# Dividing the softmax's weights before their transposition, instead of the attention's outputs

## The chip, the cores and the metric

One core of one Trainium2 chip. The metric is the device time of one execution in microseconds (us), as the median of three runs. Of the core's engines, TensorE (PE in the profile) multiplies matrices and transposes, VectorE (DVE) and ScalarE (ACT) work element by element and both read PE's results from PSUM, GpSimd (POOL) works element by element on SBUF, and SyncE (SP) starts the transfers of the weights. Each engine runs its own queue of instructions in order and waits at semaphores for the others.

## What is computed

Two transformer blocks in float32 over 512 positions of width 1024: a first block with a convolution branch, an attention with 16 heads of 64 and a feed-forward part, and a second block of two layers, one with a masked softmax attention over selected keys, one with a stick-breaking attention. The change touches the softmax of the first two attentions. Cut to that, the reference is

```
# first attention: a bias by distance, three dilated windows merged into one softmax
scores = q @ k.T - slopes * dist          # masked
m = max(scores);  p = exp(scores - m);  den = sum(p)
o = (p @ v) / den
y_b = o @ w_attn_out                      # later multiplied by a sigmoid gate

# second attention: keys selected per query
p = softmax(where(selected, q @ k.T * 0.125, -inf))
o = p @ v
y = (o * silu(g)) @ w_out_a
```

## The kernel before

Matrix products in float32 are made of three products of halves: each operand is split into a high and a low part (`h`, `l`; names ending in h and l or hi and lo), and PE runs h x h, l x h and h x l. ACT writes the high part, DVE or GpSimd subtracts it to get the low one. For weights that is `whi` on ACT and `wlo` on GpSimd (lines 119 and 123).

An attention runs over 8 pairs of heads (`pair_loop`). The queue of PE is written out by hand and goes along in slots, one for each head. In a slot PE computes, for four tiles of 128 queries, the scores of the present head (`scores`, lines 579 and 582: two products into one of two PSUM banks `s`, of 128, 256, 384 and 512 keys), the transpositions of the head before (`turn`, line 593: ten transpositions of 128x128 in three groups, into three banks `pt`), and the products of that earlier head's weights with the values (`weigh`, line 512, into the single bank `o`). Between any two of these steps stand some products of the projections for the pair after next (`pe.pull`; lines 301 to 303 and 325 to 327), which fill the time in which DVE and ACT work on the scores.

The element-wise work of a head and tile of queries: DVE takes scores and bias and writes the sum to `P` and its maximum to `nm` (line 626, one operation and a one-column read of its accumulator); ACT does the exponential in place and sums it to `den` (line 192). After the transposition ACT copies the high half to `PTh` (line 595), DVE subtracts it from `pt` to get `PTl` (line 596). When both heads of a pair are weighted, `joined` adds the two halves of `o` (ACT's copy at 518, DVE's addition at 519) into `f`.

The weights `P` are not divided by their sums. For each pair `widen` takes the reciprocals of the 2 x 4 columns of `den` (line 632) and spreads each over 64 columns of a tile `wide` (634), `denominators` transposes that tile with four PE transpositions into a bank `pt` (639), and ACT copies it to `rb`, times 0.5 (641). Then `finish` multiplies the outputs by it: in the first attention at line 943, into `o32`; in the second, line 1477 first multiplies the gate `gs` into `rb`, and 1478 the result into `f`. The 0.5 belongs to gates that are kept as twice their value.

The order on PE is fixed by the program's text. On DVE, ACT and GpSimd a scheduler decides the order when the kernel is built.

Of the kernel before, what the change touches and what calls it, by code (L numbers as in the profile page):

```python
# [10 lines left out]
F32 = mybir.dt.float32  # L11
F32R = mybir.dt.float32r
I32 = mybir.dt.int32
AF = mybir.ActivationFunctionType
OP = mybir.AluOpType
# [5 lines left out]
ND = D // 128  # L21
NT = S // 128
# [11 lines left out]
OFF = (0, 128, 384, 768)  # L34
# [11 lines left out]
FIRST = (2, 2, 3, 5)  # L46
DRAIN = (4, 1, 1, 2, 1, 1, 3)
# [101 lines left out]
def model_kernel(ctx: ExitStack, tc: tile.TileContext, x, norm1_g, w_in, gate_b, conv_w, conv_b, conv_norm_g,  # L149
                 w_conv_out, q_norm_g, k_norm_g, w_attn_out, w_out, norm2_g, w_up, ffn_conv_w, ffn_conv_b,  # L150
                 w_down, w_in_a, w_out_a, w_in_b, w_out_b, ln_g, ln_b, rope_c, rope_s, out, dbg=None):
    nc = tc.nc
# [18 lines left out]
    def ps_t():  # L171
        return ps("pt", 3)
# [42 lines left out]
    ident = const.tile([128, 128], F32, name="ident")  # L215
# [207 lines left out]
    with tc.tile_pool(name="rows", bufs=1) as rows, tc.manual_schedule(engines={  # L423
# [21 lines left out]
        for r in range(2):  # L445
            a = slice(64 * r, 64 * r + 64)
# [9 lines left out]
        p = ps_o()  # L456
# [43 lines left out]
    def tmp(pool):  # L500
        return pool.tile([128, S], F32, name="tmp", bufs={"dsa": 5, "loop1": 5, "loop3": 2, "glu": 3}[pool.name])
# [61 lines left out]
    class HeadPair:  # L563
# [2 lines left out]

        def __init__(self, tmps, pool, qk, v):
            self.tmps, self.pool, self.qk, self.v = tmps, pool, qk, v
            self.P, self.parts, self.o = {}, {}, {}

        def scores(self, r, qt):
            qs, (ks, kl) = self.qk
# [25 lines left out]
        def weigh(self, r, group):  # L598
            first, last = group == GROUPS[0], group == GROUPS[-1]
            if first:  # L600
                self.o[r] = ps_o()
            parts = {kt: self.parts[r, kt] for kt in group}
            values(self.o[r], self.v(), r, parts, group, first, last)
            if last:
                if r == 0:
                    self.f = tmp(self.tmps)
                joined(self.o[r], self.f, r)
                if r:
                    self.ended()

        def widen(self):
            pass

        def denominators(self):
            pass

    class SoftmaxPair(HeadPair):
        def __init__(self, tmps, pool, qk, v, bias, finish, scale=1.0):
# [5 lines left out]
        def weights(self, r, qt, n, sc, pp):  # L624
# [1 line left out]
            nc.vector.tensor_tensor_reduce(out=pp, in0=sc, in1=self.bias(r, qt), scale=-self.scale, scalar=3.0e38,  # L626
                                           op0=OP.add, op1=OP.min, accum_out=m)
            act(pp, pp, AF.Exp, bias=m, scale=-1.0, accum_out=d)

        def widen(self):  # L630
            rinv = self.pool.tile([128, 2, NT], F32, name="rinv", bufs=2)
            nc.vector.reciprocal(rinv, self.den)
            self.wide = tmp(self.tmps).rearrange("p (t r d) -> p t r d", t=NT, r=2)
            nc.vector.tensor_copy(self.wide, rinv.rearrange("p r t -> p t r")[:, :, :, None].to_broadcast([128, NT, 2, 64]))

        def denominators(self):
            pb = ps_t()
            for qt in range(NT):
                nc.tensor.transpose(pb[:, 128 * qt:128 * qt + 128], self.wide[:, qt].rearrange("p a b -> p (a b)"), ident)
            self.rb = tmp(self.tmps)  # L640
            nc.scalar.activation(self.rb, pb, AF.Copy, scale=0.5)

        def ended(self):
            self.finish(self.f, self.rb)

    class StickPair(HeadPair):

# [18 lines left out]
    def pair_loop(pair, stream_of, pulls, last=lambda: None):  # L666


        def slot(head, turns, weighs, widen, pulls):
            def step(fn):  # L670
                if fn is not None:
                    fn()
                    pe.pull(pulls.pop(0))

            pulls = list(pulls)
            score = [lambda qt=qt: head[0].scores(head[1], qt) for qt in range(NT)] if head else [None] * NT
            step(score[0])
            step(turns[0])
            step(score[1])
            step(turns[1])  # L680
            step(score[2])
            step(turns[2])
            step(weighs[0])
            step(score[3])
            step(weighs[1])
            step(weighs[2])
            if widen:
                widen()

        turns = weighs = [None] * 3  # L690
        for c in range(ND):
            stream_of(c)
            pr = pair(c)
            for r in range(2):
                slot((pr, r), turns, weighs, pr.widen if r else None, pulls[2 * c + r - 2 * ND] if c >= ND - 2 else pulls[0] if c or r else FIRST)
                turns = [(lambda g=g, r=r, pr=pr: pr.turn(r, g)) for g in GROUPS]
                weighs = [(lambda g=g, r=r, pr=pr: pr.weigh(r, g)) for g in GROUPS]
                if r:
                    weighs[1] = lambda pr=pr: (pr.weigh(1, GROUPS[1]), pr.denominators())
        last()  # L700
        pe.pull(DRAIN[0])
        slot(None, turns, weighs, None, DRAIN[1:])

    def value_tiles(pool, w, col, acts, puts):

# [80 lines left out]
    with tc.tile_pool(name="mix1", bufs=1) as mix1:  # L786
# [119 lines left out]
        with tc.tile_pool(name="loop1", bufs=1) as lp:  # L906
# [31 lines left out]
                pe.add(w_in, 0, 8, 3072 + 128 * c, hT, normed(1, kg))  # L938
                values_of(c, lp, w_in, 4096, hT, heads)

            def finish1(c):
                def finish(f, rb):
                    nc.vector.tensor_mul(o32[:, c, :], f, rb)
                return finish

            def pair1(c):
                B = []
                for r in range(2):
                    b = lp.tile([128, S], F32, name="B", bufs=2)
                    slope = 2.0 ** (-8.0 * (2 * c + r + 1) / NH)  # L950
                    nc.vector.scalar_tensor_tensor(b, dist, -float(np.float32(slope)), lnc, op0=OP.mult, op1=OP.add)
                    B.append(b)
                if c == ND - 1:
                    biased.add("last")
                    for fn in ready:
                        fn()
                    ready.clear()
                qk = heads.pop(c)
                return SoftmaxPair(lp, lp, (qk[0], qk[1]), lambda: qk["v"], lambda r, qt: B[r][:, 384 - 128 * qt:], finish1(c))

            ready = []

# [185 lines left out]

        return [(product or whole)(w, col + 128 * c, acts, done(c)) for c in cs]

    def gated(pool, into, f, c, already, scale=1.0):

        def parts():
            if not already:
                nc.vector.tensor_mul(f, f, gs[c])
            h, l = act_pair(pool, "og", ND)
            nc.scalar.activation(h, f, AF.Copy, scale=scale)
            nc.vector.scalar_tensor_tensor(l, f, scale, f32(h), op0=OP.mult, op1=OP.subtract)
            into.append((h, l))

        if already or c in gs:
            parts()
        else:
            waiting[c] = parts
# [199 lines left out]
    with tc.tile_pool(name="dsa", bufs=1) as dp:  # L1364
# [101 lines left out]
        with tc.tile_pool(name="loop2", bufs=1) as lp:  # L1466
            for g in gprods[3:]:
                pe.skewed(g)
            heads2(0)
            pe.finish()  # L1470
            heads2(1)
            pe.pull(LEAD[1] - 24)

            def finish2(c):
                def finish(f, rb):
                    if c in gs:
                        nc.vector.tensor_mul(rb, gs[c], rb)
                    nc.vector.tensor_mul(f, f, rb)
                    gated(dp, og, f, c, c in gs)
                return finish  # L1480

            def pair2(c):
                qk = heads.pop(c)
                return SoftmaxPair(dp, lp, (qk[0], qk[1]), lambda: qk["v"],
                                   lambda r, qt: maskb[:, OFF[qt]:OFF[qt] + 128 * (qt + 1)], finish2(c), 0.125)

            def stream2(c):
                if c + 2 < ND:
                    heads2(c + 2)
                elif c + 2 == ND:  # L1490
                    outs.append(Between(w_out_a, og, xS, kept))
                    outs[0].early()
                else:
                    outs[0].next()

            pair_loop(pair2, stream2, PULLS[1], lambda: outs[0].late())
            pe.finish()
            act_tables(LN_EXP)
# [9 lines left out]
    with tc.tile_pool(name="stick", bufs=1) as dp:  # L1508
        heads = {}
        og = []  # L1510
# [18 lines left out]
        with tc.tile_pool(name="loop3", bufs=1) as lp:  # L1529
            act_tables("sigmoid_and_others")  # L1530

            def pair3(c):
                qk = heads.pop(c)
                return StickPair(lp, lp, (qk[0], qk[1]), lambda: qk["v"], lambda f: gated(dp, og, f, c, False, 0.5))

            def last_e():
                es.append(dp.tile([128, S], F32, name="e", bufs=ND - 1) if es else keep.tile([128, S], F32, name="rc2"))
                return es[-1]

            es = []  # L1540

            def stream3(c):
                if c + 2 < ND:
                    heads3(lp, c + 2)
                    for g in gprods[slice(*GATES3[c + 2])]:
                        pe.skewed(g)
                elif c + 2 == ND:
                    outs.append(Last(w_out_b, og, xS, last_e))
                    outs[1].early()
                else:  # L1550
                    outs[1].next()

            heads3(lp, 0)
            heads3(lp, 1)
            pe.pull(LEAD[2])
            pair_loop(pair3, stream3, PULLS[2], lambda: outs[1].late())
            pe.finish()
            act_tables(LN_EXP)
# [27 lines left out]
```

## Time and profile before

| what | value |
|---|---|
| median of three runs | 1601.13 us (1597.56 to 1601.93) |
| profiled execution: its time | 1601.03 us |
| its span, first to last instruction | 1598.9 us |
| first attention's pairs | about 202 to 405 us |
| second attention's pairs | about 1046 to 1232 us |

The profile is of one execution, and its span lies 2.1 us inside that execution's time. Busy times are unions per engine; PE's instructions overlap one another, so their start times tell more than their lengths. A row by stretches gives the stretch's bounds and length in us, then the busy time and the number of instructions of PE, of PE's weight loads (PEld), of DVE, ACT and POOL, the granted share of PE's full clock, the share of the DMA engines and GB/s. A row of a group gives line, engine, operation, tiles and shapes with their count, then the busy time in us and the mean of one in ns, then the idle time ahead of them and what ended it. A row of the chain gives start and length in us.

### The profile page before, as it was taken

To read this page: it belongs to the slowest core of one execution; us is meant where nothing else is said; L and a number is where in the kernel's file an instruction comes from. 1 tells how busy PE (TensorE), PEld (TensorE's weight loads), DVE (VectorE), ACT (ScalarE), POOL (GpSimd) and SP (SyncE) were. 2 spreads that over 40 slices of the span, in tenths; PEclk is the share of its full clock that TensorE was granted. 3 is DMA by queue.
4 is the path that set the end of the run, shared out by engine and by line. 5 is a ranking of instruction groups with operands and counts; after the bars stand their busy time and mean duration, and the time that the engine had idled before them with its cause. 6 is when DMAs were issued, how large, how long until landed. Compare 5 with 4: busy or idle time off the path is not lost.

```text
span 1598.9 us, 21378 instructions
## 1 busy us (share of the span) xinstructions
PE 1527.2 (96%) x7870; PEld 1296.7 (81%) x7870; DVE 1121.4 (70%) x1837; ACT 845.4 (53%) x1524; POOL 806.5 (50%) x680
## 2 busy tenths in 40 slices
PE   7999799998999999999999999999999789999996
PEld 6877688887878888888888887888887678888885
DVE  8998777776166467727735669988887765777764
ACT  4455787777552444424333444366766345666652
POOL 3789944332744653454444474445442875334324
PEclk9999899999999999999999999999999899999998
DMA  4323212221233423343333242322220313212212
GB/s 149 88 87 98 86 54 73 60 67 40 67 105 105 126 86 92 93 118 91 90 110 89 84 125 66 80 80 66 67 67 14 92 40 106 67 54 80 67 52 80
DMA packets 234604, 130.37 MB, mean 82 GB/s; under 512 B 5206, under 2 KB 232774, under 8 KB 234500
## 3 DMA queue, kind: packets, MB, share of 16 engines
q1 hardware_dynamic: 234356, 128.75, 27.7%
q8 instruction: 62, 1.02, 0.3%
q14 instruction: 42, 0.34, 0.1%
q10 hardware_dynamic: 144, 0.26, 0.0%
HBM read 126.90 MB, written 2.10 MB: 81 GB/s over the span
## 4 chain that ended last, share of the span: by engine, by line
PE 57%; DVE 23%; ACT 7%; POOL 5%; issue 5%; DMA 2%; DVEq 0%; SPq 0%; ACTq 0%; POOLq 0%
PE pj L301 10%; PE pj L302 9%; PE pj L303 9%; PE s L302 5%; PE s L303 5%; PE s L301 5%; DVE pt L831 5%; PE o L512 2%; POOL wlo L123 2%; PE pt L593 2%; PE pj L325 2%; PE pj L327 2%; PE pj L326 2%; POOL S L837 2%; DVE score L1442 1%
## 5 line engine op out<-in xcount | busy, mean ns | idle before, releaser
L123 POOL TENSOR_TENSOR wlo<-wraw,whi 128x256 fp32r<-128x256 f32 (+2 forms) x548 | 653.8, 1218 | 684.4 <-ACT whi L119 639.0
L301 PE MATMUL pj<-Ah,whi 128*128 128x512 f32 (+3 forms) x896 | 362.2, 404 | 15.2 <-DVE v L718 9.8
L119 ACT CAST whi<-wraw 128x1024 fp32r<-128x1024 f32 (+3 forms) x255 | 243.8, 965 | 224.3 <-PE pj L302 82.1
L303 PE MATMUL pj<-Ah,wlo 128*128 128x512 f32 (+3 forms) x896 | 350.4, 391 | 2.5 <-POOL wlo L123 2.5
L302 PE MATMUL pj<-Al,whi 128*128 128x512 f32 (+3 forms) x896 | 350.7, 391 | 0.0
L301 PEld LDWEIGHTS pj<-Ah,whi 128*128 128x128 f32 (+1 forms) x896 | 171.2, 191 | 41.9 <-issue 9.1
L303 PEld LDWEIGHTS pj<-Ah,wlo 128*128 128x128 f32 (+1 forms) x896 | 170.3, 190 | 39.1 <-POOL wlo L123 3.4
L302 PEld LDWEIGHTS pj<-Al,whi 128*128 128x128 f32 (+1 forms) x896 | 171.1, 191 | 24.4
L301 PE MATMUL s<-Ah,whi 128*128 128x512 f32 (+1 forms) x352 | 135.8, 386 | 4.0 <-ACT Ah L1298 4.0
L302 PE MATMUL s<-Al,whi 128*128 128x512 f32 (+1 forms) x352 | 135.7, 386 | 3.6 <-DVE Al L1299 3.6
L303 PE MATMUL s<-Ah,wlo 128*128 128x512 f32 (+1 forms) x352 | 135.6, 385 | 1.0 <-POOL wlo L123 1.0
L831 DVE SCALAR_TENSOR_TENSOR pt<-S,cw,pt 128x496 f32<-128x496 f32 (+19 forms) x180 | 124.8, 738 | 6.4 <-ACT pt L824 3.8
L325 PE MATMUL pj<-whi,Ah 128*128 128x256 f32 x384 | 112.4, 293 | 1.4 <-DVE q L533 1.4
L596 DVE TENSOR_TENSOR PTl<-pt,PTh 128x512 fp32r<-128x512 f32 x144 | 86.0, 598 | 32.9 <-ACT PTh L595 31.9
L327 PE MATMUL pj<-whi,Al 128*128 128x256 f32 x384 | 108.4, 282 | 0.0
L326 PE MATMUL pj<-wlo,Ah 128*128 128x256 f32 x384 | 108.3, 282 | 0.0
L192 ACT ACTIVATE P<-P,nm 128x128 f32<-128x128 f32 (+3 forms) x128 | 72.0, 563 | 63.2 <-DVE nm L626 61.9
L744 DVE SCALAR_TENSOR_TENSOR u<-ur,fw,u 128x511 f32<-128x511 f32 x44 | 74.9, 1705 | 37.5 <-ACT u L743 37.5
L837 POOL TENSOR_TENSOR S<-S,o 128x511 f32<-128x511 f32 (+29 forms) x60 | 78.2, 1317 | 15.4 <-ACT o L836 14.3
L595 ACT CAST PTh<-pt 128x512 fp32r<-128x512 f32 x144 | 73.1, 513 | 19.6 <-PE pt L593 19.1
L302 PEld LDWEIGHTS s<-Al,whi 128*128 128x128 f32 x352 | 67.8, 193 | 17.1 <-DVE Al L1299 4.5
L301 PEld LDWEIGHTS s<-Ah,whi 128*128 128x128 f32 x352 | 67.9, 193 | 17.1 <-ACT Ah L1298 4.6
(334 smaller groups left out, 3250.8 us busy)
## 6 DMA issues: line engine op xcount, KB each, us to landing
wraw<-in_w_in_dram SPq DMA_DIRECT2D x56, 512.0 KB
wraw<-in_w_up_dram SPq DMA_DIRECT2D x44, 512.0 KB
wraw<-in_w_in_a_dram SPq DMA_DIRECT2D x36, 512.0 KB
wraw<-in_w_in_b_dram SPq DMA_DIRECT2D x32, 512.0 KB
wraw<-in_w_down_dram SPq DMA_DIRECT2D x16, 512.0 KB
wraw<-in_w_attn_out_dram SPq DMA_DIRECT2D x8, 512.0 KB
wraw<-in_w_conv_out_dram SPq DMA_DIRECT2D x8, 512.0 KB
wraw<-in_w_out_dram SPq DMA_DIRECT2D x8, 512.0 KB
```

Source lines behind the costliest of these rows:

```text
L119: nc.scalar.copy(h, s)
L123: nc.gpsimd.tensor_sub(l[:, k], s[:, k], h[:, k].bitcast(F32))
L301: nc.tensor.matmul(o, hv[:, k, :], ah, start=first, stop=False)
L302: nc.tensor.matmul(o, hv[:, k, :], al, start=False, stop=False)
L303: nc.tensor.matmul(o, lv[:, k, :], ah, start=False, stop=last)
L325: nc.tensor.matmul(o, ah, hv, start=k == 0, stop=False)
L326: nc.tensor.matmul(o, ah, lv, start=False, stop=False)
L327: nc.tensor.matmul(o, al, hv, start=False, stop=k == 7)
L596: nc.vector.tensor_sub(l[:, :at], pt[:, :at], f32(h)[:, :at])
L744: nc.vector.scalar_tensor_tensor(u[:, 1:], v[:, :S - 1], fw[:, 1, j:j + 1], u[:, 1:], op0=OP.mult, op1=OP.add)
L831: nc.vector.scalar_tensor_tensor(o, a, w, o, op0=OP.mult, op1=OP.add)
L837: nc.gpsimd.tensor_add(o, o, t)
```

## The change

Right after the exponential, DVE takes the reciprocal of the one column of `den` in place and multiplies the tile's `P` by it and by 0.5, in place. `widen`, `denominators`, `rb` and the multiplications by `rb` go. In the first attention the outputs are joined directly in `o32`; in the second `gated` multiplies them by the gate as it already does for the third attention. The third attention's arithmetic is as before.

```diff
     class SoftmaxPair(HeadPair):
         def weights(self, r, qt, n, sc, pp):
             m, d = self.nm[:, r, qt:qt + 1], self.den[:, r, qt:qt + 1]
...
             act(pp, pp, AF.Exp, bias=m, scale=-1.0, accum_out=d)
-
-        def widen(self):
-            rinv = self.pool.tile([128, 2, NT], F32, name="rinv", bufs=2)
-            nc.vector.reciprocal(rinv, self.den)
-            self.wide = tmp(self.tmps).rearrange("p (t r d) -> p t r d", t=NT, r=2)
-            nc.vector.tensor_copy(self.wide, rinv.rearrange("p r t -> p t r")[:, :, :, None].to_broadcast([128, NT, 2, 64]))
-
-        def denominators(self):
-            pb = ps_t()
-            for qt in range(NT):
-                nc.tensor.transpose(pb[:, 128 * qt:128 * qt + 128], self.wide[:, qt].rearrange("p a b -> p (a b)"), ident)
-            self.rb = tmp(self.tmps)
-            nc.scalar.activation(self.rb, pb, AF.Copy, scale=0.5)
+            nc.vector.reciprocal(d, d)
+            nc.vector.tensor_scalar(pp, pp, d, 0.5, op0=OP.mult, op1=OP.mult)
 
         def ended(self):
-            self.finish(self.f, self.rb)
+            self.finish(self.f)
...
-            def finish1(c):
-                def finish(f, rb):
-                    nc.vector.tensor_mul(o32[:, c, :], f, rb)
-                return finish
...
+                pr.f = o32[:, c, :]
+                return pr
...
-    def gated(pool, into, f, c, already, scale=1.0):
+    def gated(pool, into, f, c, scale=1.0):
 
         def parts():
-            if not already:
-                nc.vector.tensor_mul(f, f, gs[c])
+            nc.vector.tensor_mul(f, f, gs[c])
...
-            def finish2(c):
-                def finish(f, rb):
-                    if c in gs:
-                        nc.vector.tensor_mul(rb, gs[c], rb)
-                    nc.vector.tensor_mul(f, f, rb)
-                    gated(dp, og, f, c, c in gs)
-                return finish
```

On PE the order changes only by what goes. One of the eight places in the first attention, where a pair's second head is weighted, had before (`o` is the bank of the outputs, `tmp` the tile `wide`):

```order
L512 MATMUL o<-PTh,v 128x384
L512 MATMUL o<-PTl,v 128x384
L512 MATMUL o<-PTh,v 128x128
L512 MATMUL o<-PTl,v 128x128
L639 MATMUL pt<-ident,tmp 128x128 x4
L325 MATMUL pj<-whi,Ah 128x256
L326 MATMUL pj<-wlo,Ah 128x256
```

and has now:

```order
L512 MATMUL o<-PTh,v 128x384
L512 MATMUL o<-PTl,v 128x384
L512 MATMUL o<-PTh,v 128x128
L512 MATMUL o<-PTl,v 128x128
L325 MATMUL pj<-whi,Ah 128x256
L326 MATMUL pj<-wlo,Ah 128x256
```

The four transpositions are gone, and nothing else moved on PE.

On DVE, in the second attention, the second head of the third pair (profile before: from 1109.95 us) had this order. ISA is the operation of line 626 and its accumulator read, `pt` and `PTh` are read for `PTl`, `q` belongs to the projections:

```order
L626 ISA P,nm<-s,maskb 128x256
L626 ISA nm 128x1
L1381 TENSOR_TENSOR tmp<-tmp 128x512
L596 TENSOR_TENSOR PTl<-pt,PTh 128x512
L626 ISA P,nm<-s,maskb 128x384
L626 ISA nm 128x1
L533 SCALAR_TENSOR_TENSOR q_9652<-tmp,q_9652 64x512
L596 TENSOR_TENSOR PTl<-pt,PTh 128x256
L626 ISA P,nm<-s,maskb 128x512
```

and has now (line 620 is the old 626, 1356 the old 1381):

```order
L620 ISA P,nm<-s,maskb 128x256
L620 ISA nm 128x1
L1356 TENSOR_TENSOR tmp<-tmp 128x512
L596 TENSOR_TENSOR PTl<-pt,PTh 128x512
L623 RECIPROCAL den<-den 128x1
L533 SCALAR_TENSOR_TENSOR q_9694<-tmp,q_9694 64x512
L624 TENSOR_SCALAR P<-P,den 128x256
L620 ISA P,nm<-s,maskb 128x384
L620 ISA nm 128x1
L533 SCALAR_TENSOR_TENSOR q_9695<-tmp,q_9695 64x512
L596 TENSOR_TENSOR PTl<-pt,PTh 128x256
L623 RECIPROCAL den<-den 128x1
```

A reciprocal and a multiplication now stand ahead of the next maximum and of the next `PTl`; the reciprocal waits for ACT's exponential.

On DVE, in the first attention, the second head of the third pair (profile before: from 268.0 us) had this order; `tmp<-tmp,vec` and `kl` belong to the projections:

```order
L626 ISA P,nm<-s,B 128x256
L626 ISA nm 128x1
L920 SCALAR_TENSOR_TENSOR tmp<-tmp,vec 128x512
L596 TENSOR_TENSOR PTl<-pt,PTh 128x512
L560 TENSOR_TENSOR kl_1595<-tmp,k_2440 64x512
L560 TENSOR_TENSOR kl_1596<-tmp,k_2441 64x512
L626 ISA P,nm<-s,B 128x384
L626 ISA nm 128x1
L596 TENSOR_TENSOR PTl<-pt,PTh 128x512
L596 TENSOR_TENSOR PTl<-pt,PTh 128x256
```

and has now (line 899 is the old 920):

```order
L620 ISA P,nm<-s,B 128x256
L620 ISA nm 128x1
L899 SCALAR_TENSOR_TENSOR tmp<-tmp,vec 128x512
L624 TENSOR_SCALAR P<-P,den 128x128
L596 TENSOR_TENSOR PTl<-pt,PTh 128x512
L560 TENSOR_TENSOR kl_1595<-tmp,k_2454 64x512
L560 TENSOR_TENSOR kl_1596<-tmp,k_2455 64x512
L623 RECIPROCAL den<-den 128x1
L620 ISA P,nm<-s,B 128x384
L620 ISA nm 128x1
L624 TENSOR_SCALAR P<-P,den 128x256
L596 TENSOR_TENSOR PTl<-pt,PTh 128x512
```

Here a multiplication stands ahead of the first `PTl`, and a reciprocal and a second multiplication ahead of the next; the reciprocal of the first tile has moved ahead of the piece shown.

## Rows read from the trace of the kernel before

**Rows 1.** the page: engines; granted clock of PE in 40 slices, tenths

```profile
PE 1527.2 (96%) x7870; PEld 1296.7 (81%) x7870; DVE 1121.4 (70%) x1837; ACT 845.4 (53%) x1524; POOL 806.5 (50%) x680
...
PEclk9999899999999999999999999999999899999998
```

**Rows 2.** stretches, a pair of heads each

```profile
251.50:279.80 28.30, 28.11 (x168) 24.29 (x167) 22.11 (x44) 22.58 (x47) 10.56 (x12) 1.00 0.23 66
1046.40:1069.90 23.50, 23.38 (x136) 20.20 (x134) 20.54 (x46) 15.48 (x34) 10.93 (x12) 1.00 0.25 68
1069.90:1092.90 23.00, 22.83 (x149) 20.58 (x148) 16.64 (x41) 16.26 (x39) 9.68 (x11) 1.00 0.25 69
1092.90:1120.00 27.10, 26.93 (x159) 23.16 (x157) 25.09 (x52) 18.03 (x40) 15.14 (x16) 1.00 0.22 59
```

**Rows 3.** the chain of waits, 1104 to 1124 us

```profile
1107.59 0.54 DVE ogl L1158
...
1111.17 0.60 DVE PTl L596
...
1113.47 0.39 PE o L512
```

**Rows 4.** PE in time order, 262 to 289; in brackets idle before

```profile
273.00 0.44 PE L512 MATMUL o<-PTl,v 128*128 128x384 f32 x1 [0.19 <-DVE PTl L596]
...
282.84 0.41 PE L593 MATMUL pt<-ident,P 128*128 128x128 f32 x2 [0.35 <-DVE PTl L596]
```

**Rows 5.** PE in order of time, 281 to 288

```profile
286.68 0.63 PE L639 MATMUL pt<-ident,tmp 128*128 128x128 f32 x4
287.06 0.36 PE L325 MATMUL pj<-whi,Ah 128*128 128x256 f32 x1
287.26 0.28 PE L326 MATMUL pj<-wlo,Ah 128*128 128x256 f32 x1
287.38 0.28 PE L327 MATMUL pj<-whi,Al 128*128 128x256 f32 x1
```

**Rows 6.** the chain of waits, 398 to 412

```profile
402.91 0.60 ACT tmp L641
...
404.87 0.70 DVE o L943
```

**Rows 7.** groups of DVE by line and shape

```profile
L626 DVE DVE_READ_ACCUMULATOR2_ANT nm<- 128x1 f32 x128 | 10.4, 81 | 0.0
...
L634 DVE COPY tmp<-rinv 128x512 f32<-128x512 f32 x16 | 9.5, 594 | 0.2
...
L1477 DVE TENSOR_TENSOR tmp<-S,tmp 128x512 f32<-128x512 f32 x8 | 5.5, 692 | 8.0 <-ACT tmp L641 8.0
...
L632 DVE RECIPROCAL rinv<-den 128x8 f32<-128x8 f32 x16 | 3.2, 201 | 9.1 <-ACT P L192 9.1
```

**Rows 8.** same view: single-source operations of DVE

```profile
L805 DVE TENSOR_SCALAR t<-t 128x512 f32<-128x512 f32 x2 | 0.8, 421 | 0.0
...
L1457 DVE TENSOR_SCALAR score<-tmp,wi 128x384 f32<-128x384 f32 x1 | 0.6, 596 | 0.0
L442 DVE TENSOR_SCALAR ones_d<-zero 128x128 fp32r<-128x128 f32 x1 | 0.6, 567 | 0.0
L1443 DVE TENSOR_SCALAR maskb<-score 128x256 f32<-128x256 f32 x1 | 0.6, 555 | 0.0
...
L1443 DVE TENSOR_SCALAR maskb<-score 128x384 f32<-128x384 f32 x1 | 0.4, 361 | 0.0
L1457 DVE TENSOR_SCALAR score<-tmp,wi 128x256 f32<-128x256 f32 x1 | 0.3, 338 | 0.0
...
L444 DVE TENSOR_SCALAR ones_b<-zero 128x128 fp32r<-128x128 f32 x1 | 0.3, 299 | 0.0
```

**Rows 9.** instructions of line 634: duration ns min/median/max

```profile
L634 DVE COPY tmp<-rinv x16: 407/426/958, 227.3 to 1224.6; 128x512 f32<-128x512 f32 x16
```

**Rows 10.** both attentions: sum of the stretches 195:410 and 1040:1230

```profile
sum 405.00, PE 392.86 PEld 339.04 DVE 308.39 ACT 294.81 POOL 169.28; mean PE 196.43 PEld 169.52 DVE 154.20 ACT 147.41 POOL 84.64
```

More of the change, by code (lines that the diff above doesn't have):

```diff
@@ L568, in __init__ @@
             self.tmps, self.pool, self.qk, self.v = tmps, pool, qk, v
-            self.P, self.parts, self.o = {}, {}, {}
+            self.P, self.parts, self.o, self.f = {}, {}, {}, None
         def scores(self, r, qt):
@@ L604, in weigh @@
             if last:
-                if r == 0:
+                if r == 0 and self.f is None:
                     self.f = tmp(self.tmps)
@@ L609, in weigh @@
                     self.ended()
-        def widen(self):
-            pass
-        def denominators(self):
-            pass
     class SoftmaxPair(HeadPair):
@@ L628, in weights @@
             act(pp, pp, AF.Exp, bias=m, scale=-1.0, accum_out=d)
-        def widen(self):
-            rinv = self.pool.tile([128, 2, NT], F32, name="rinv", bufs=2)
-            nc.vector.reciprocal(rinv, self.den)
-            self.wide = tmp(self.tmps).rearrange("p (t r d) -> p t r d", t=NT, r=2)
-            nc.vector.tensor_copy(self.wide, rinv.rearrange("p r t -> p t r")[:, :, :, None].to_broadcast([128, NT, 2, 64]))
-        def denominators(self):
-            pb = ps_t()
-            for qt in range(NT):
-                nc.tensor.transpose(pb[:, 128 * qt:128 * qt + 128], self.wide[:, qt].rearrange("p a b -> p (a b)"), ident)
-            self.rb = tmp(self.tmps)
-            nc.scalar.activation(self.rb, pb, AF.Copy, scale=0.5)
+            nc.vector.reciprocal(d, d)
+            nc.vector.tensor_scalar(pp, pp, d, 0.5, op0=OP.mult, op1=OP.mult)
         def ended(self):
-            self.finish(self.f, self.rb)
+            self.finish(self.f)
     class StickPair(HeadPair):
@@ L666, in pair_loop, with slot @@
     def pair_loop(pair, stream_of, pulls, last=lambda: None):
-        def slot(head, turns, weighs, widen, pulls):
+        def slot(head, turns, weighs, pulls):
             def step(fn):
@@ L686, in slot @@
             step(weighs[2])
-            if widen:
-                widen()
         turns = weighs = [None] * 3
@@ L694, in pair_loop @@
             for r in range(2):
-                slot((pr, r), turns, weighs, pr.widen if r else None, pulls[2 * c + r - 2 * ND] if c >= ND - 2 else pulls[0] if c or r else FIRST)
+                slot((pr, r), turns, weighs, pulls[2 * c + r - 2 * ND] if c >= ND - 2 else pulls[0] if c or r else FIRST)
                 turns = [(lambda g=g, r=r, pr=pr: pr.turn(r, g)) for g in GROUPS]
                 weighs = [(lambda g=g, r=r, pr=pr: pr.weigh(r, g)) for g in GROUPS]
-                if r:
-                    weighs[1] = lambda pr=pr: (pr.weigh(1, GROUPS[1]), pr.denominators())
         last()
         pe.pull(DRAIN[0])
-        slot(None, turns, weighs, None, DRAIN[1:])
+        slot(None, turns, weighs, DRAIN[1:])
     def value_tiles(pool, w, col, acts, puts):
@@ L958, in pair1 @@
                 qk = heads.pop(c)
-                return SoftmaxPair(lp, lp, (qk[0], qk[1]), lambda: qk["v"], lambda r, qt: B[r][:, 384 - 128 * qt:], finish1(c))
+                pr = SoftmaxPair(lp, lp, (qk[0], qk[1]), lambda: qk["v"], lambda r, qt: B[r][:, 384 - 128 * qt:], lambda f: None)
+                pr.f = o32[:, c, :]
+                return pr
             ready = []
@@ L1159, in parts @@
             into.append((h, l))
-        if already or c in gs:
+        if c in gs:
             parts()
@@ L1484, in pair2 @@
                 return SoftmaxPair(dp, lp, (qk[0], qk[1]), lambda: qk["v"],
-                                   lambda r, qt: maskb[:, OFF[qt]:OFF[qt] + 128 * (qt + 1)], finish2(c), 0.125)
+                                   lambda r, qt: maskb[:, OFF[qt]:OFF[qt] + 128 * (qt + 1)],
+                                   lambda f: gated(dp, og, f, c), 0.125)
             def stream2(c):
@@ L1533, in pair3 @@
                 qk = heads.pop(c)
-                return StickPair(lp, lp, (qk[0], qk[1]), lambda: qk["v"], lambda f: gated(dp, og, f, c, False, 0.5))
+                return StickPair(lp, lp, (qk[0], qk[1]), lambda: qk["v"], lambda f: gated(dp, og, f, c, 0.5))
             def last_e():
```

## The prediction

> **What bounds the kernel now.** I read the page first. TensorE (PE) is busy 96% of the span and VectorE (DVE) 70%; the granted clock is at the upper level, 2.4 GHz, nearly everywhere [rows 1]. So the starting guess is that TensorE sets the time and that a removed matmul is worth its own length. The share is an average, so next I cut both attentions into their pairs of heads, where the edit lies [rows 2]. There TensorE is idle for 0.1 to 0.4 us of a full pair, but the rows differ in DVE: in the first attention it is idle 28.3 - 22.1 = 6.2 us of a pair, in the second 6.35 us of one (23.0 - 16.65) and 2.0 us of the next (27.1 - 25.1). I call a pair of the last kind heavy; such are those that start at 1092.9, 1143.0 and, shortened, 1193.2.
>
> Then I asked which engine sets the end inside a heavy pair. The chain of waits runs on DVE from 1107.59 to the end of a PTl at 1111.77, without another engine between, and hands over to PE only at the value product at 1113.47 [rows 3]: here DVE already sets the time, and a microsecond laid on its queue is a microsecond. In the first attention the chain turns to DVE in places: at 273.0 and 282.84 PE waits 0.19 and 0.35 us for the subtraction that makes PTl [rows 4]. What stands ahead of a PTl on DVE's queue is therefore late for PE at once.
>
> **The change part by part.** *PE.* Four transpositions and one bank of pt go per pair. In the stream the four start at 286.68, the next product at 287.06, and that product's successor 0.20 us later where such products otherwise follow by 0.12 [rows 5]. So a pair saves 0.38 + 0.08 = 0.46 us, sixteen pairs 7.4 us, as long as PE is what sets the time.
>
> *ACT.* One copy from PSUM of 0.58 us goes per pair; its length stands in the chain at 402.91 [rows 6]. ACT is idle over 5 us of a pair [rows 2], so I cost this at nothing, except at the end of the first attention, below.
>
> *DVE, removed.* Per pair one reciprocal of eight columns (201 ns), the widening copy (594 ns) and one multiplication (692 ns) [rows 7]: 1.49 us. In the second attention the wait of the multiplication at L1477 for ACT goes too: 8.0 us in seven times.
>
> *DVE, added.* Per head four reciprocals of one column and four in-place multiplications of 128, 256, 384 and 512 columns. No row has either exactly. For the reciprocal the same operation on eight columns (201 ns) is the upper end, and the one-column read of an accumulator (81 ns) the lower [rows 7]; I take 0.20, being the same operation. For the multiplication the nearest rows are single-source operations of the same widths, and they come in two levels: 299, 338, 361 and 421 ns, in sum 1.42 us [rows 8], or 567, 555 and 596 ns [rows 8] and for 512 columns the longest widening copy, 958 ns [rows 9], in sum 2.68 us. That copy shows what separates the levels: 407 ns at least, 958 at most, and the long ones lie inside stretches in which GpSimd works. GpSimd is busy 37 to 56% of these pairs [rows 2], so I take 1.42 + 0.42 x 1.26 = 1.95 us. The four multiplications wait for their reciprocals (0.03 us each), while the following instruction may overlap by 0.07: minus 0.16. A head gains 0.80 + 1.95 - 0.16 = 2.6 us, a pair 5.2; by the lower ends 2 x (0.32 + 1.42 - 0.16) = 3.2, by the upper ones 2 x (0.80 + 2.68 - 0.16) = 6.6. Net of what goes, a pair puts **3.7 us** more on DVE (1.7 to 5.1), sixteen pairs 59 us.
>
> The Trainium skill's page "SBUF — State Buffer", section "SBUF: two separate sides", has a rule for the two levels: VectorE in a two-port mode and GpSimd share one pair of ports as an exclusive lock, and the later one waits until the other's whole instruction is over. The copy's 407 and 958 ns agree with it. [...]
>
> *Where it lands.* The queue now holds, ahead of PTl, a reciprocal that waits for ACT's Exp and a multiplication; behind them queue the maximum of the next scores, which frees one of two banks s, and PTl, for which PE waits.
> Heavy pair: net 3.7 us against 2.0 us of idle time. Most of that idle time is waits for ACT that stay in place; I count 1.0 us as usable, so +2.7. Three such pairs: +8.1. The first pair (1046.4) has 3.0 us idle, of which I count 1.9: +1.8. The last pair, which drains: +0.8. The three light pairs have 6.35 us idle for 3.7 us of work; PE stays the bound and gains 0.46 each: -1.4. Second attention: +9.3.
> First attention: 6.2 us idle for 3.7, so on average DVE has room, and the places decide. At 265 to 274 a reciprocal and a multiplication stand newly ahead of each of two PTl, about 1.2 us against a slack of 0.7 us or less; at 276 to 282.8 the lag left over, some 1.1 us, meets the transposition that waits already. I take 1.65 us for such a detour; the chain has it again 52 us later, and I add 1.0 for the attention's start and 2.0 for the shorter slots after 356: together +6.3 (2 x 1.65 + 1.0 + 2.0). PE's saving is 8 x 0.46 = -3.7. At the end of this attention the chain runs transpositions, ACT's copy of them, copy, addition, multiplication [rows 6]: the multiplication of 0.70 us goes and the copy of the outputs starts earlier by the 0.60 us of ACT, -1.4 with the gap. First attention: +1.2.
> Sum: 9.3 + 1.2 = **+10.5 us**. The profiled execution took 1601.03 us, 2.1 above its span and 0.1 under the median of 1601.13, so I forecast 1601 + 10.5, that is **1611 us**.
>
> **The rivals.** A change under 0.3% (4.8 us) can't be told from none here.
> *A, PE stays the bound:* DVE's idle time swallows everything, the pairs gain 7.4 us and the end of the first attention 1.4: 1592 us. For it: DVE has 308 of 405 us busy over both attentions [rows 10], so 97 us of room for 59. Against it: the room isn't where the work falls [rows 3, 4].
> *B, a draw:* the heavy pairs cost half (some +5), the first attention gains 3: near 1601 us. This is what a cheaper reciprocal (0.08 us) with mostly undisturbed multiplications gives: net 1.7 to 2.2 us per pair.
> *C, DVE sets the pace everywhere:* multiplications at the upper level (net 5.1) and 0.4 us of waiting for Exp at each of eight reciprocals of a pair. Then full pairs of the first attention need 5.1 + 3.2 against 6.0 us, +2.3 in each of seven (+16, less 1.4 at the end); heavy pairs +4.3 (three, with 3.4 and 2.6 at the ends: +19): 1635 us. It decides from the point where the waits for Exp exceed about 0.3 us each.
> *D, GpSimd becomes late:* if each added multiplication holds GpSimd up for its own length, 128 of them take some 50 us from it, and the low halves of the weights (wlo) come late. GpSimd is idle over 10 us of most pairs [rows 2], so only where blocks crowd; at a guess from that, 7 us above the main case: 1618 us.
>
> **How the numbers follow.** Main case (between 1604 and 1624) 0.54, A 0.14, B 0.18, C 0.09, D 0.05. The forecast is the main case's 1611 us. The range from 1595 to 1628 takes in B and D, leaves out most of A and all of C, about 0.2. Faster by over 0.3% is A: 0.14; within 0.3% is B: 0.18; slower is the rest: 0.68. Reading the main case alone, its own range is 1604 to 1624.
>
> **What would show it.** In the profile after: DVE's busy time over the two attentions up by about 59 us, with the new multiplications between 0.3 and 1.0 us and in two levels; no L639 transpositions; the pairs that start the second attention's heavy slots longer by 2 to 4 us with PE waiting there for PTl and nm, the light ones shorter by about half a microsecond; the first attention nearly as long as before; and beyond the attentions nothing changed. The prediction is wrong if the heavy pairs don't grow (A, B: then the waits I counted as fixed were slack), if the reciprocals stand idle for Exp by more than 0.3 us each (C), or if the wait of matmuls for wlo grows inside the attentions (D).

## The result, and the profile after

The changed kernel takes 1611.77 us (median; 1611.48 to 1613.52), the kernel before on the same chip 1601.51: a ratio of 1.0072, 95% interval 1.0054 to 1.0089. It is slower by 10.3 us where +10.5 was forecast. The profiled execution spans 1609.7 us against 1598.9.

The page of after, sections 1 and 4 (section 4: the chain that ended last, by engine and by line), to be held against [rows 1]:

```profile
PE 1523.9 (95%) x7806; PEld 1291.0 (80%) x7806; DVE 1163.9 (72%) x2045; ACT 837.2 (52%) x1508; POOL 806.1 (50%) x680
...
PE 55%; DVE 27%; ACT 8%; issue 5%; POOL 4%; DMA 1%; DVEq 0%; SPq 0%; ACTq 0%; POOLq 0%
```

The same line of the chain before:

```profile
PE 57%; DVE 23%; ACT 7%; POOL 5%; issue 5%; DMA 2%; DVEq 0%; SPq 0%; ACTq 0%; POOLq 0%
```

DVE's busy time is up by 42.5 us, and its share of the chain has grown from 23 to 27%, while PE's fell from 57 to 55%. PE does less and the kernel is longer, so PE now waits. The view of stretches shows where; these are the four of [rows 2], cut at the same matmuls:

```profile
253.00:281.60 28.60, 27.61 (x164) 24.03 (x163) 25.39 (x59) 22.00 (x46) 10.57 (x12) 1.00 0.23 65
1049.00:1074.00 25.00, 23.67 (x134) 19.78 (x133) 22.39 (x60) 15.96 (x36) 10.55 (x11) 1.00 0.24 64
1074.00:1096.50 22.50, 22.50 (x147) 20.46 (x146) 19.85 (x54) 15.48 (x38) 11.39 (x14) 1.00 0.26 71
1096.50:1125.60 29.10, 26.45 (x152) 22.44 (x151) 27.62 (x69) 18.79 (x41) 14.93 (x15) 1.00 0.20 55
```

The stretch in the first attention has grown from 28.3 to 28.6 us, the second attention's first pair from 23.5 to 25.0, the heavy pair from 27.1 to 29.1; the light pair has shrunk from 23.0 to 22.5, and PE is idle for none of it. In the heavy pair PE is idle for 29.10 - 26.45 = 2.65 us. What it waits for over the whole kernel (engine, line, waited for: us in total, times, longest):

```profile
PE o L512 <- DVE PTl L596: 11.2, 14, 1.6
...
PE o L512 <- ACT PTh L595: 4.8, 3, 3.1
...
PE s L579 <- DVE nm L620: 3.4, 3, 1.3
...
PE pj L303 <- POOL wlo L123: 2.5, 2, 2.1
```

Before, these waits were 1.9, 2.1, 1.4 and 2.5 us; the first and the third read then:

```profile
PE o L512 <- DVE PTl L596: 1.9, 8, 0.6
...
PE s L579 <- DVE nm L626: 1.4, 5, 0.4
```

Over the whole kernel PTl is what comes late most. In the heavy pair above, the maximum `nm` is as late as PTl, and the two waits are nearly all of PE's idle time there:

```profile
PE o L512 <- DVE PTl L596: 1.3, 1, 1.3
PE s L579 <- DVE nm L620: 1.3, 1, 1.3
```

The chain of waits through that heavy pair (start, us, what) shows what stands ahead of PTl on DVE; its piece of before is [rows 3]:

```profile
1110.24 0.16 DVE den L623
1110.40 0.59 DVE tmp L1130
1110.99 0.20 DVE P L624
1111.19 0.03 issue
1111.22 0.63 DVE PTl L596
...
1117.38 0.35 DVE P L624
1117.73 0.47 DVE P L620
1118.20 0.03 issue
1118.24 0.69 DVE q L533
1118.94 0.43 DVE PTl L596
1119.37 0.04 issue
1119.41 0.39 PE o L512
```

The new reciprocal (L623) and multiplication (L624) lie in the chain ahead of PTl, and the value product at 1119.41 starts when PTl ends.

What the added operations cost on DVE, by shape (count | busy us, mean ns | idle before and what ended it):

```profile
L623 DVE RECIPROCAL den<-den 128x1 f32<-128x1 f32 x128 | 20.2, 158 | 24.5 <-ACT P L192 23.9
...
L624 DVE TENSOR_SCALAR P<-P,den 128x512 f32<-128x512 f32 x32 | 18.1, 566 | 0.9
L624 DVE TENSOR_SCALAR P<-P,den 128x384 f32<-128x384 f32 x32 | 17.5, 547 | 0.7
...
L624 DVE TENSOR_SCALAR P<-P,den 128x128 f32<-128x128 f32 x32 | 12.6, 392 | 0.8
L624 DVE TENSOR_SCALAR P<-P,den 128x256 f32<-128x256 f32 x32 | 12.5, 390 | 0.5
```

A head's four multiplications take 0.566 + 0.547 + 0.390 + 0.392 = 1.895 us (1.95 forecast), a reciprocal 0.158 (0.20 forecast). In all 20.2 + 60.7 = 80.9 us come onto DVE, and 16 x 1.49 = 23.8 go: 57 us net by lines (59 forecast). The page's 42.5 is less mostly because DVE's instructions overlap in the records: the lengths of all of them, added up, grow by 53.3 us, from 1197.6 to 1250.9.

### The profile page after: what moved, and what is told of

The parts are those of the page before. It is cut to its first block, busy times and chain, and to the rows that moved or that the text cites. A ratio compares the mean times of both kernels' runs of the same rounds, so it can differ in the third digit from the quotient of the medians.

```text
span 1609.7 us, 21424 instructions
## 1 busy us (share of the span) xinstructions
PE 1523.9 (95%) x7806; PEld 1291.0 (80%) x7806; DVE 1163.9 (72%) x2045; ACT 837.2 (52%) x1508; POOL 806.1 (50%) x680
## 4 chain that ended last, share of the span: by engine, by line
PE 55%; DVE 27%; ACT 8%; issue 5%; POOL 4%; DMA 1%; DVEq 0%; SPq 0%; ACTq 0%; POOLq 0%
PE pj L301 9%; PE pj L302 9%; PE pj L303 9%; PE s L302 5%; PE s L303 5%; PE s L301 5%; DVE pt L810 5%; PE pt L593 2%; POOL wlo L123 2%; PE o L512 2%; POOL S L816 2%; DVE P L624 2%; DVE P L620 1%; PE pj L325 1%; DVE PTl L596 1%
## 5 line engine op out<-in xcount | busy, mean ns | idle before, releaser
L593 PE MATMUL pt<-ident,P 128*128 128x128 f32 x480 | 78.3, 276 | 3.6 <-DVE P L624 1.8
```

The lines of the kernel that those rows point to most:

```text
L593: nc.tensor.transpose(pt[:, at:at + 128], self.P[r][:, k0:k0 + 128], ident)
```

## The experiments

My theory: the removal gains what PE and DVE no longer do, and the multiplications take it back, because in the heavy pairs they stand ahead of PTl and the next maximum on a queue without room. The rivals: DVE's new waits for Exp cost more than the work; the amount of work on DVE counts, wherever it stands; one place in the first attention makes most of the loss. The twelve kernels ran in three groups of four, each group with its own runs of the kernel before (1600.94, 1600.94 and 1601.22 us).

**The outputs undivided.** From the changed kernel:

```diff
-            nc.vector.reciprocal(d, d)
-            nc.vector.tensor_scalar(pp, pp, d, 0.5, op0=OP.mult, op1=OP.mult)
```

> The outputs of the first two attentions are left undivided: neither the old division nor the new reciprocals and multiplications. Theory (the removal gains what TensorE no longer does, and the added VectorE work takes more than that back): 16 x 0.46 = 7.4 us for TensorE, 1.4 at the end of the first attention, and in three heavy pairs the 1.49 us that VectorE no longer has, less the 0.46 counted already, some 3: 1601.5 - 11.8 = 1590 us, between 1587 and 1594. Rival (the transpositions were hidden, or the removal itself disturbs): 1597 us or more.

Measured: 1590.03 us, ratio 0.9927 (0.9914 to 0.9941). The theory's 1590. The light pair and the heavy pair here:

```profile
1065.10:1087.60 22.50, 22.50 (x148) 20.45 (x147) 15.29 (x37) 15.23 (x38) 9.81 (x13) 1.00 0.25 71
1087.60:1113.70 26.10, 26.01 (x153) 22.54 (x152) 22.89 (x49) 18.22 (x40) 14.46 (x15) 1.00 0.22 61
```

The light pair is as long as in the changed kernel, 22.5 us, though DVE has 4.6 us less to do: the added work is free there. The heavy pair is 3.0 us shorter than in the changed kernel, with 22.9 us of DVE's work where that has 27.6. So the change is a gain of 10.9 us by what it removes and a loss of some 21 us by what it adds: 10.9 + 10.3 = 21.2 from the kernel before in each group, 1611.77 - 1590.03 = 21.7 directly, but across two groups.

That the number came out so exactly is luck. From pair to pair the removal did other things than I had summed: the last two light pairs gain 0.9 us each where 0.46 was reckoned, the heavy pairs 0.6 each where it was 1.49, and the first attention's seventh pair is 3.3 us longer than before (25.9 against 22.5), although nothing was added.

**Each attention alone.** From the kernel before; a flag chooses the way for each SoftmaxPair, and the two steps of the division are left out where it is set:

```diff
             act(pp, pp, AF.Exp, bias=m, scale=-1.0, accum_out=d)
+            if self.early:
+                nc.vector.reciprocal(d, d)
+                nc.vector.tensor_scalar(pp, pp, d, 0.5, op0=OP.mult, op1=OP.mult)
```

> The change in the second attention alone. Theory (the heavy pairs of the second attention carry most of the loss): the second attention's +8.2 us, so 1609.7 us, between 1608 and 1612. Rival (most of the loss is the 3.1 us wait in the first attention, and what follows from it): 1605 us or less.

> The change in the first attention alone. Theory (the first attention costs little in the end): +2.6 us as the trace after shows it at the second attention's start, 1604 us, between 1602 and 1606. Rival (the 4 us given back after the first attention, by stretches at the lower clock that fall elsewhere, are an accident of the one execution): 1606 to 1609 us.

Measured: the second attention alone 1608.36 us, ratio 1.0044 (1.0032 to 1.0057), so +7.4; the first alone 1604.71 us, ratio 1.0024 (1.0015 to 1.0033), so +3.8. Together 11.2, the whole change within its interval. The second attention carries two thirds, as the theory has it; the first costs more than I had forecast. But not all of that lies in the first attention. In the profiled execution of the first alone PE is 1.3 us late where the second attention starts, as against 3.9 us at the end of the span; the rest comes in the second attention's drain, which this kernel leaves as it was, and behind it: 1.6 us at 1220 to 1235 us, where the clock is at its lower level for 3.4 us and wasn't before.

**One cast back at its old place.** In the trace after, PE waits 3.1 us for a PTh in the first attention's seventh pair. ScalarE's timeline there:

```profile
377.68 1.28 ACT L201 ACT_TABLE_LOAD   x1
378.98 2.53 ACT L558 CAST k<-tmp 64x512 fp32r<-64x512 f32 x4
381.52 0.61 ACT L192 ACTIVATE P<-P,nm 128x384 f32<-128x384 f32 x1
...
382.70 0.36 ACT L595 CAST PTh<-pt 128x256 fp32r<-128x256 f32 x1
```

Before the change this cast stood ahead of the table load. The undivided kernel has the cast behind the table load too and waits 3.1 us for it, and so do the two kernels below with the reciprocals alone (3.0 us) and with GpSimd (2.9 us): the place on the queue came with what the change removes, not with the work that it adds. The experiment raises the cast's priority in that one place, so that the scheduler puts it there again:

```diff
-            nc.scalar.copy(h[:, :at], pt[:, :at])
+            with later(-50 if (r, group) == self.soon else 0):
+                nc.scalar.copy(h[:, :at], pt[:, :at])
```

> The changed kernel, with one cast (the 256 columns of PTh at 382.7 us) at the place on ScalarE's queue that it had before the change, ahead of the table load and the casts of k. Theory (the 3.1 us wait there is ScalarE's new order): the wait goes, 1611.8 - 3.1 = 1608.7 us, between 1607.5 and 1610. Rival (VectorE would have been late for the same matmul anyway, so another wait takes its place): within 1 us of 1611.8.

Measured: 1609.28 us, ratio 1.0047 (1.0035 to 1.0060). The cast has moved:

```profile
377.07 0.35 ACT L597 CAST PTh<-pt 128x256 fp32r<-128x256 f32 x1
377.44 1.28 ACT L201 ACT_TABLE_LOAD   x1
```

The wait of 3.1 us is gone. PE's lag behind the kernel before at 390 us (matched matmul by matmul) falls from 6.3 to 3.8 us; but where the second attention starts it is 2.2 us, against 2.6. The median is 2.5 us under the changed kernel's first measurement and 3.5 under its repeat below, the profiled span only 0.4; that execution is the slowest of its five (1607.07 to 1611.07). So the new order explains the wait, and between 0.4 and 3.5 us of the total; the runs don't settle which.

**Reciprocals alone.** From the changed kernel, the line of the multiplication taken out.

> The changed kernel with its reciprocals but without its multiplications, so that the weights stay undivided; it has the same 128 waits of VectorE for Exp as the change. Theory (the added work counts by its length): the reciprocals are 128 x 0.158 = 20.2 of 80.9 us of added work, a quarter of the 21.8 us that lie between the undivided kernel and the changed one, 1590.0 + 5.4 = 1595.4 us, between 1593 and 1598. Rival (what costs is that VectorE's queue now waits for Exp at every reciprocal): over half of the 21.8 us, 1601 us or more.

Measured: 1592.21 us, ratio 0.9945 (0.9932 to 0.9957): 2.2 us above the undivided kernel, under the theory's range and less even than the 5.4 by length. The waits for Exp are all there (DVE's own waits: us, times, longest; in the changed kernel they are 23.9 us in 42 times):

```profile
DVE den L623 <- ACT P L192: 30.5, 53, 1.0
```

and cost next to nothing. The rival of waits for Exp falls. What the multiplications cost is 1612.77 - 1592.21 = 20.6 us (the repeat of the changed kernel, below, against this run), a third of their length of 60.7.

**The multiplications on GpSimd.**

```diff
-            nc.vector.tensor_scalar(pp, pp, d, 0.5, op0=OP.mult, op1=OP.mult)
+            nc.gpsimd.tensor_scalar(pp, pp, d, 0.5, op0=OP.mult, op1=OP.mult)
```

> The change, but with the multiplications on GpSimd instead of VectorE. By GpSimd's 512 columns in 1.29 us a head's 1280 columns take 3.2 us, a pair's 6.4, against 10 to 16 us that GpSimd is idle in a pair. Theory (what costs is the work on VectorE's queue): as with the reciprocals alone, 1595 to 1599 us, faster than before. Rival (GpSimd becomes late, with the low halves of the weights or with P itself): 1603 us or more.

Measured: 1596.83 us, ratio 0.9975 (0.9965 to 0.9985), faster than both kernels. GpSimd takes 0.52 to 0.88 us for each, as means by width, 83 us in all:

```profile
L624 POOL TENSOR_SCALAR P<-P,den 128x512 f32<-128x512 f32 x32 | 28.0, 875 | 29.5 <-DVE den L623 21.8 <-PE pj L302 4.4 <-PE pt L593 2.2
...
L624 POOL TENSOR_SCALAR P<-P,den 128x128 f32<-128x128 f32 x32 | 16.7, 523 | 23.6 <-DVE den L623 22.9 <-PE s L582 0.7
```

and PE's waits show what is left of the cost (the transpositions wait for P, and wlo is no later than before):

```profile
PE pt L593 <- POOL P L624: 7.2, 13, 1.8
...
PE pj L303 <- POOL wlo L123: 2.5, 2, 2.1
```

**The multiplications on ScalarE.** It leaves out the factor of a half.

```diff
-            nc.vector.tensor_scalar(pp, pp, d, 0.5, op0=OP.mult, op1=OP.mult)
+            act(pp, pp, AF.Copy, scale=d)
```

> The change, but with the multiplications on ScalarE instead of VectorE, as a copy with a factor per row. By the Exp of the same widths (0.40, 0.51, 0.62 and 0.71 us) a pair puts 4.5 us more on ScalarE, which is idle 5 to 9 us of a pair. Theory (what costs is the work on VectorE's queue): 1595 to 1600 us. Rival (ScalarE's own order: the copy stands ahead of PTh and of the next Exp, and its wait for the reciprocal holds the queue): 1605 us or more.

Measured: 1615.34 us, ratio 1.0091 (1.0078 to 1.0105): my theory's number missed by 15 us, the rival's side holds. DVE is as free as with GpSimd, but the transpositions now wait for ScalarE:

```profile
PE pt L593 <- ACT P L192: 15.9, 13, 3.0
```

To take work off the late engine isn't enough; the engine that gets it must have room at these places. How much of it is ScalarE's load and how much its order wasn't told apart.

**The changed kernel again**, in the same group as the last three.

> The changed kernel once more, beside these. Every theory: 1611.8 us, between 1610 and 1613; were it 1609.3, the one cast that the run with the earlier order moved would have gained nothing.

Measured: 1612.77 us, ratio 1.0071 (1.0059 to 1.0084).

**Light pairs or heavy pairs.** The same number of multiplications, 24, goes to GpSimd, once in the light pairs and once in the heavy pairs of the second attention (c in (1, 3, 5), or c in (2, 4, 6)); all others stay on DVE:

```diff
-            nc.vector.tensor_scalar(pp, pp, d, 0.5, op0=OP.mult, op1=OP.mult)
+            self.by(r, qt).tensor_scalar(pp, pp, d, 0.5, op0=OP.mult, op1=OP.mult)
...
+                if c in (1, 3, 5):
+                    pr.by = lambda r, qt: nc.gpsimd
```

> The changed kernel, with the multiplications of three light pairs of the second attention (the second, fourth and sixth) on GpSimd. Theory (the place decides: the light pairs have room on VectorE, and take 24.24 us with the multiplications on either engine): no gain, 1612.3 us, between 1611 and 1613.5. Rival (the amount of work on VectorE decides, wherever it stands): 24 of 128 multiplications, which cost 20.1 us in all, so 3.8 us less, 1608.5 us or lower.

> The changed kernel, with the multiplications of the three heavy pairs of the second attention (the third, fifth and seventh) on GpSimd: as many as in the run of the light pairs. Theory (the place decides): the heavy pairs fall back from 27.3 to 25.0 us, twice, and the last from 20.9 to 19.2, 6.3 us less, 1606 us, between 1604.5 and 1607.5. Rival (the amount decides): 3.8 us less, 1608.5 us, as for the light pairs.

Measured: light 1611.91 us, ratio 1.0067 (1.0054 to 1.0079), no gain; heavy 1604.39 us, ratio 1.0024 (1.0014 to 1.0034), 7.5 us less than the run of the light pairs beside it, where the theory had 6.3. The heavy pair in the run of the light pairs, and in the run of the heavy pairs:

```profile
1099.30:1128.50 29.20, 26.50 (x153) 22.47 (x153) 27.72 (x65) 18.39 (x40) 14.92 (x15) 1.00 0.20 55
```

```profile
1099.90:1126.80 26.90, 26.36 (x153) 22.58 (x152) 24.28 (x58) 18.05 (x40) 19.60 (x22) 1.00 0.21 59
```

It is 29.2 us with its multiplications on DVE and 26.9 with them on GpSimd; DVE has 3.4 us less to do in it.

The totals alone don't carry the conclusion. In both traces PE is already 5.2 and 6.1 us late where the second attention starts, against 2.6 us in the changed kernel, though up to there all three have the same instructions. In the run of the light pairs that loss is made up in part in the last pair's drain, which costs 1.1 us there instead of 3.0. So its total is the changed kernel's in part by accident. The lengths of the pairs, from a pair's first score matmul to the next pair's, settle it. The light pairs take 24.5, 24.2 and 24.2 us with their multiplications on GpSimd, and 24.6, 24.2 and 24.2 in the changed kernel with them on DVE. The heavy pairs take 25.0, 25.0 and 19.2 us with theirs on GpSimd, and 27.3, 27.3 and 20.9 in the changed kernel, 6.2 us more in sum, as the theory had it. The drain behind them costs 1.0 us instead of 3.0. The place decides, and the rival of the amount falls.

**Two attempts to improve on GpSimd.** In the first the multiplications of 512 columns go back to DVE, in the whole first attention and in the second's first pair; in the second kernel only those of the second's first pair:

```diff
+                pr.by = lambda r, qt: nc.vector if c == 0 and qt == 3 else nc.gpsimd
```

> The multiplications on GpSimd, but those of 512 columns on VectorE in the first attention and, in the second, in its first pair alone. Theory (TensorE's waits of 0.3 to 0.6 us for these tiles at the starts of the first attention's pairs, and of 1.8 us in the second's first pair, come from GpSimd being slower or behind four blocks of weights; VectorE has room there): 1.4 us from the first pair and some 1.5 from the others, 1594 us, between 1593 and 1595.5. Rival (VectorE's added work costs in the first attention as it did in the changed kernel): 1597 us or more.

> The multiplications on GpSimd, except those of 512 columns in the first pair of the second attention, which VectorE does. Theory (the 1.8 us wait there is the multiplication that stands behind four blocks of weights on GpSimd's queue): 1.4 us less than with GpSimd throughout, 1595.4 us, between 1594.5 and 1596. Rival (another wait takes its place in the same pair): 1596.8 us.

Measured: 1599.74 us, ratio 0.9990 (0.9981 to 0.9999), and 1596.53 us, ratio 0.9970 (0.9959 to 0.9982). Both theories missed, and both rivals hold. The first shows that work on DVE costs in the first attention too: 3.2 us over the second kernel, which differs by the 16 multiplications there alone. In the traces 1.3 us of this come in the first six pairs; the rest comes from the seventh on, where the clock is at its lower level for 13.6 us against 6.8. In the second the wait of 1.8 us is gone:

```profile
PE pt L593 <- DVE P L625: 0.4, 1, 0.4
PE o L512 <- DVE PTl L596: 0.2, 1, 0.2
```

but two shorter ones have come, the pair is 0.6 us shorter instead of 1.4, and the total can't be told from GpSimd throughout. These two, near 1596.7 us, are the fastest that compute the whole.

## Why the prediction was right, point by point

**The sum** was right (+10.5 against +10.3), and its main mechanism is shown: PTl and the next maximum late behind the new work in heavy pairs. The split was less good: +9.3 for the second attention and +1.2 for the first, against 7.4 (5.1 to 9.1) and 3.8 (2.4 to 5.3) with each alone, and 8.2 and 2.6 in the trace after, taken where the second attention starts. The errors cancelled, and that the sum came within 0.2 us is luck. Lengths of pairs below run from a pair's first score matmul to the next pair's.

**The light pairs** were mis-sized: -0.46 each forecast, -0.5, -0.9 and -0.9 measured. By the undivided kernel's matmuls against those of before, the second light pair saves 0.38 us at the transpositions, as in [rows 5], and 0.4 us more at its scores of 384 columns: before, the widening copy (0.95 us at 1117.98) stood on DVE ahead of a maximum, for which PE then waited. I had costed the removed DVE work as room and not as a wait of PE.

**The heavy pairs**: +2.7 each forecast (8.1 for three), +2.3, +2.3 and +1.5 measured (6.1). The step "I count 1.0 us as usable" was nearly right. The first pair: +1.8 forecast, +1.5 measured.

**The last pair's drain**: +0.8 forecast, +3.0 measured in the trace after. PE waits there five times for PTl, 3.0 us in all, and the granted clock falls to its lower level (1.2 GHz) for two stretches of 3.4 us that no other pair of this attention has (the column behind POOL's):

```profile
1214.00:1222.00 8.00, 6.29 (x25) 4.58 (x24) 6.95 (x24) 4.94 (x13) 1.28 (x1) 0.79 0.00 0
1222.00:1230.00 8.00, 6.33 (x40) 5.03 (x39) 7.52 (x25) 6.21 (x17) 0.96 (x1) 1.00 0.00 0
1230.00:1238.00 8.00, 7.17 (x28) 5.47 (x28) 5.03 (x14) 3.65 (x7) 0.31 (x1) 0.79 0.01 2
```

With the change in the second attention alone PE waits as long, the clock stays at the upper level, and the drain costs 1.1 us. I hadn't reckoned with the clock.

**The first attention**: the step "2.0 for the shorter slots after 356" failed. The seventh pair alone grew by 5.6 us. PE's waits in it went from 2.2 us (for k and for a maximum) to 5.4: 1.6 for PTl and 3.8 for PTh; the rest is the clock, at its lower level for some 6 us of the pair (0.89 over it, 1.00 before). Before, a stretch of 6.8 us at the lower level begins just behind this pair, and so 1.6 us of the lag are gone again by 390 us. Most of the two waits isn't the added work: the undivided kernel, which has neither reciprocals nor multiplications, waits 1.2 us for PTl and 3.4 for PTh in the same pair. The multiplication of 384 columns that stands ahead of that PTl takes 0.41 us. The wait for PTh came from a place where I looked only at ScalarE's idle time and costed it "at nothing"; the change gave ScalarE another order, which can be read from the instruction lists before any run. That the error stayed small in the total has another reason: of the lag of 6.7 us at 470 us, 2.7 are given back by 480. There PE waits for ScalarE's th in any case, 2.4 us before and 1.3 after, and what follows ran at the lower clock for 3.4 us before and not after. Another 1.4 us come back at 958 to 970, where the lower clock lasts 3.4 us instead of 6.8. This isn't dependable: the run of the light pairs, with the same order of instructions in the first attention, waits 3.0 us for th and then has 6.8 us at the lower clock:

```profile
470.00:478.00 8.00, 5.01 (x21) 3.84 (x20) 8.00 (x9) 3.49 (x6) 3.97 (x2) 0.87 0.22 66
478.00:486.00 8.00, 8.00 (x27) 6.33 (x26) 5.12 (x8) 2.98 (x4) 2.73 (x2) 0.71 0.35 105
```

and starts the second attention 5.2 us late instead of 2.6. Why the clock falls in one and not in the other stays open.

**The unknown prices.** The multiplications were the main one: 1.95 us a head from the two levels of [rows 8, 9], 1.895 measured. The lower level is there: the 83 of the 128 that no GpSimd instruction overlaps take 0.28, 0.35, 0.42 and 0.49 us by width. The upper is no second level but a wait: the other 45 take 0.53, 0.54, 0.80 and 0.68 us on the mean, and up to 1.85. The Trainium skill, "SBUF — State Buffer", section "SBUF: two separate sides", describes the pair of ports that VectorE and GpSimd share as an exclusive lock: the engine whose instruction starts first keeps it for the whole instruction, and the other waits. The trace agrees on both sides; for instance:

```profile
1102.90 0.73 POOL L123 TENSOR_TENSOR wlo<-wraw,whi 128x256 fp32r<-128x256 f32 x1 [4.73 <-ACT whi L119]
1103.01 0.84 DVE L624 TENSOR_SCALAR P<-P,den 128x384 f32<-128x384 f32 x1
1103.59 0.85 POOL L123 TENSOR_TENSOR wlo<-wraw,whi 128x256 fp32r<-128x256 f32 x1
```

The multiplication starts inside GpSimd's first subtraction and ends 0.22 us after it, so that it takes 0.84 us instead of 0.42; the second subtraction starts inside the multiplication and ends 0.59 us after it. The 23 multiplications that start 0.2 us or more before a GpSimd instruction's end are over 0.08, 0.15, 0.22 and 0.28 us after that end, by width. Of the 38 subtractions of 256 columns that start inside a multiplication, 28 end 0.59 to 0.62 us after it and take up to 1.01 us, where the 43 that no VectorE instruction overlaps take 0.72 to 0.75 us. Yet the mean of all 418 is 859 ns after and 858 before: before the change, too, all but 48 of them overlapped some VectorE instruction.

**The rivals.** A (DVE's room swallows everything) would have been right for the removal alone, which gains 10.9 us. B is refuted by the heavy pairs. C is refuted by the reciprocals alone: 2.2 us for 128 waits, and in the changed kernel they stand idle for Exp by 23.9 / 128 = 0.19 us each, under the 0.3 from which C decides. D is refuted: the new multiplications do hold single subtractions up, but GpSimd's are no longer on the mean, and wlo costs PE 2.5 us before and after.

## What to carry to other kernels

Price an edit in the stretch in which the engine that gets the work has no room: 24 multiplications were free in three pairs and cost 6.2 us in three others, with some 2 us more in the drain behind them. When a change takes work off the busiest engine, ask first what it puts on the next in line, and then whether a third engine with room at those places can have it: on GpSimd, where each multiplication took longer than on VectorE, the same change became a gain of 0.25%. And compare the order of instructions on every engine, those too on which the edit lays nothing.

## What the runs showed of the hardware

A short wait of PE can cost more than its length by a stretch at the lower clock that follows, and such stretches come and go between kernels with the same instructions at that place: 2.7 us were given back at 472 to 480 us in the changed kernel, and 1.8 us lost there in another with the same order. GpSimd did the in-place multiplication of 512 columns in 0.88 us, where its subtraction of 512 columns takes 1.29. VectorE's in-place multiplications and GpSimd's subtractions wait for each other's end: 0.42 us became 0.84 on VectorE, 0.74 became up to 1.01 on GpSimd, while GpSimd's mean stayed at 0.86 us.
